# Four plain pairs instead of six, a packed block and closings set aside: one change to a weight-gradient kernel

## The chip, the cores and the metric

The kernel runs on one NeuronCore of a Trainium2 chip. The engines named here are TensorE (PE: matmuls, and PEld: its weight loads), VectorE (DVE), ScalarE (ACT), GpSimd (POOL) and SyncE (SP). The metric is the device time of one execution in microseconds (us), from runs of which the median counts.

## What is computed

```
batch, m, k, n = 16, 512, 1024, 768
grad_weight = np.einsum('bmk,bmn->kn', input, grad_output)     # float32 in, float32 out
```

Batch and m together are one contraction over 8192 rows: out (1024 x 768) = X^T G, with X (8192 x 1024) and G (8192 x 768).

## The kernel before

**Pairs.** The 8192 rows are cut into 32 pairs u = 0 to 31 of 256 rows each. A pair's X and G come by DMA from GpSimd's queue, which turns f32 into bf16 on the way; only the first 128 rows (and the X of the second 128) come as f32 on the queues of SP and ACT and are rounded on the chip (round_by). From pair 3 on (MERGED) a pair is one DMA for G (L159) and one for X (L160); earlier pairs come in halves (L164, L166). The pool "pairs" has room for 14 (PAIRS_HELD).

**Blocks.** The output is cut into four blocks: A (first half of K, left half of N), B (first half of K, right), C (second half of K, left), D (second half of K, right). Each is 512 x 384 and is made of four row groups q of 128 x 384, called A0 to A3 and so on.

**Plain and Winograd pairs.** LOADS gives the kind of every pair. A plain pair ("s") is two items of 128 rows, and each item costs one matmul (128 x 128 weights, 384 moving columns) for each of the 16 row groups: 32 matmuls. A pair of the other kind ("P") is treated as a 2 x 2 by 2 x 2 block product by the Winograd form of Strassen's scheme: 7 products instead of 8, 28 matmuls. Its products are collected in A, B and C and in four shared sums called 1, 5, 6 and 7, each with four row groups as well. It needs six sums on DVE ahead of its products: sum_x stages 0, 1, 2 (L190, L192, L194) and sum_g stages 0, 1, 2 (L200, L202, L204), in the order that the plan gives. Their results xe and ge lie in the pool "sums" (SUMS_HELD = 10). D collects only from plain pairs. At the end the shared sums are added into A, B, C and D (SHARED, and two subtractions at the closing of 5).

**Banks.** PSUM has eight banks. A row group that is being collected occupies one. Those that are not have their running sum in SBUF: acc for A to D, macc for 1, 5, 6 and 7. A row group comes back in one of two ways: ACT copies its running sum into a bank (fill, L281) and the matmuls add to it there, or it starts from zero and its closing adds. A closing takes it out: ACT copies (L334), DVE copies (L336), or DVE adds the bank to the running sum (L338). The last closing of a row group adds a shared sum on DVE (L318, L314, L315) and stores it to DRAM, on SP's queue. The very last block is filled in two banks, 256 and 128 columns, so that its first piece can be closed while the second is multiplied; the 256-column piece is stored on ACT's queue.

**Order.** PE, DVE, ACT and GpSimd run in the order of the program, and that is the order of PLAN, a list of 1069 tokens written out by hand or by a planner. `A3@1.2`: two matmuls of A3, opened in bank 1. `C0.1`: one more of C0. `fB2@1`: fill B2 into bank 1. `vA3`, `cA2`: close by DVE or by ACT. `g1.6`, `x0.6`: a stage of the sums of pair 6. `r0`: a rounding of the first rows. The loop at the end of the function (L343 to L359) issues the tokens one by one. In this plan four row groups at a time stay in their banks over long stretches (A0, A1, C0, C1 at first), and banks 1, 2, 6 and 7 rotate.

Of the kernel before, what the change touches and what calls it, by code (L numbers as in the profile page):

```python
# [9 lines left out]
P = 128  # L10

LOADS = "ssssssPPPPPPPPPPPPPPPPPPPPPPPPPs"
# [10 lines left out]
    "A0@0.1 A3@1.1 A2@2.1 C3@7.1 vA3 C2@6.1 cA2 C0@4.1 C1@5.1 r0 cC3 A1@3.1 vC2 B2@1.1 D2@2.1 D1@7.1 cB2 "  # L23
    "r1 D3@6.1 r2 r3 vD2 D0@1.2 r4 A0.1 vD3 C1.1 cD1 B1@2.2 vD0 A1.1 B3@7.2 cB1 B0@6.2 vB3 D1@1.1 D2@2.1 "
    "cB0 C0.1 vD1 A3@7.2 fC2@6 vD2 C1.1 A1.1 fB2@1 A0.1 vA3 C2.2 C3@2.2 cC2 A2@7.2 vC3 B2.2 fD3@6 C0.1 "
    "vA2 D2@2.2 cB2 D3.3 vD2 B1@1.2 cD3 B0@7.2 vB1 D0@2.2 fD1@6 C0.1 vB0 C1.1 fB3@1 D1.3 vD0 fA3@7 B3.3 "
    "vD1 A3.2 cB3 C3@6.2 vA3 C2@2.2 fA2@1 A0.2 vC3 fB2@7 A2.3 vC2 fB0@6 B2.3 vA2 B0.2 vB2 fD3@1 D2@2.2 "
    "A1.3 vB0 fB1@7 vD2 D3.2 fD0@6 B1.2 cD3 B3@2.1 D0.2 vB1 fA3@1 C1.2 vB3 C0.2 cD0 A3.1 fD1@7 C2@2.1 "
    "C3@6.1 vA3 A0.3 vC2 fA2@1 D1.3 vC3 A3@2.2 cD1 A2.2 vA3 B0@6.2 fB1@7 A1.2 vA2 fB2@2 B1.2 vB0 B3@1.2 "
    "cB1 B2.2 vB3 C2@6.2 fC3@7 C0.2 vB2 fD0@1 C3.2 vC2 D2@2.2 cC3 D0.2 vD2 D3@6.2 fA2@7 C1.4 vD0 fA3@2 "  # L30
    "vD3 fB0@1 A2.2 A3.2 cA2 B1@6.2 vA3 B0.2 fB2@7 A0.2 vB1 cB0 B3@2.2 fC2@6 B2.2 vB3 C3@1.2 cB2 A1.2 vC3 "
    "fD2@2 C0.2 C2.2 fD1@7 D2.4 fB1@1 vC2 D1.4 cD2 D3@6.4 cD1 D0@2.1 g0.6 D0.3 vD3 A1.2 B1.1 g1.6 fB0@6 "
    "B1.1 vD0 A2@7.2 cB1 C0.1 g2.6 C0.1 A0.2 fA3@2 vA2 C1.2 fB3@1 x0.6 C1.1 A3.3 fC2@7 B0.1 x1.6 B0.1 cA3 "
    "C2.2 x2.6 cB0 C2.1 B3.3 vC2 fC3@6 B2@2.2 g0.7 cB3 B2.1 C3.3 fB0@7 vB2 C0.1 fA2@1 A1.1 g1.7 73@2.1 "
    "vC3 B0.1 A2.1 c73 A0.1 vB0 11@6.1 cA2 13@2.1 g2.7 13.1 c11 10@7.1 x0.7 10.1 12@1.2 c13 71@6.1 v10 "
    "A0.1 c12 50@2.2 v71 51@7.2 c50 72@1.1 x1.7 72.1 c51 70@6.1 g0.8 70.1 63@2.1 c72 x2.7 63.1 A1.1 c70 "
    "C0.1 g1.8 11@1.1 v63 C1.1 fA2@7 60@6.2 g2.8 62@2.2 v11 c60 A2.2 c62 x0.8 A1.1 C2@1.2 cA2 C3@6.2 x1.8 "
    "52@2.3 vC2 53@7.2 x2.8 c52 53.1 61@1.1 g0.9 61.2 c53 A0.1 vC3 fB1@2 C1.1 A3@7.1 g1.9 A3.1 c61 C0.1 "
    "B1.3 vA3 f13@6 B0@1.1 g2.9 B0.1 cB1 73@7.2 x0.9 13.2 f12@2 C1.1 v73 A1.1 c13 12.2 x1.9 C0.1 f71@6 "
    "50@7.2 vB0 A0.1 c12 71.1 x2.9 71.2 f72@1 g0.10 B2@2.3 c71 v50 72.2 fB3@6 g1.10 63@7.2 c72 vB2 B3.2 "  # L40
    "g2.10 B3.1 11@2.3 v63 cB3 10@1.1 x0.10 fC3@7 10.2 A0.1 fA2@6 v11 C1.1 C3.2 x1.10 A2.2 f51@2 v10 A1.1 "
    "C0.1 cC3 51.1 g0.11 51.2 cA2 60@1.1 x2.10 60.2 f70@7 g1.11 62@6.3 c51 v60 70.2 g2.11 fC2@1 70.1 v62 "
    "A3@2.3 c70 x0.11 C2.3 f73@6 A0.1 vA3 f53@7 73.2 cC2 x1.11 73.1 53.3 v73 f52@1 61@2.2 x2.11 c53 61.1 "
    "52.1 g0.12 fB1@6 52.2 C0.1 v61 fB0@7 C1.1 B1.1 g1.12 B1.2 c52 B0.1 g2.12 B0.2 cB1 12@1.2 x0.12 cB0 "
    "12.1 13@2.3 f71@6 v12 A1.2 f72@7 x1.12 71.3 f50@1 v13 72.2 c71 x2.12 72.1 50.1 g0.13 f63@2 50.2 A0.1 "
    "c72 B2@6.3 v50 fB3@7 63.1 g1.13 63.2 vB2 fA2@1 B3.2 g2.13 c63 B3.1 A2.1 x0.13 A2.2 fC3@6 C0.2 cB3 "
    "vA2 C1.2 10@2.1 f11@7 x1.13 10.2 f51@1 C3.1 x2.13 C3.2 g0.14 11.3 cC3 v10 51.3 c11 g1.14 70@6.3 "
    "f60@2 v51 A0.1 f62@7 A1.1 g2.14 60.3 v70 fA3@1 62.1 x0.14 62.2 c60 A3.3 fC2@6 v62 52@2.2 x1.14 cA3 "
    "52.1 C2.2 f53@7 x2.14 C2.1 A0.1 g0.15 f73@1 A1.1 53.3 cC2 v52 73.1 g1.15 73.2 f61@6 v53 B0@2.3 c73 "
    "g2.15 61.3 fB1@7 vB0 C0.1 f12@1 C1.1 x0.15 C1.1 c61 B1.3 f13@2 x1.15 12.3 vB1 50@6.2 c12 x2.15 50.1 "  # L50
    "13.1 g0.16 fB3@7 13.2 A0.1 f72@1 v50 A1.1 B3.2 c13 g1.16 B3.1 72.1 g2.16 72.2 cB3 10@2.2 c72 71@6.3 "
    "v10 fB2@1 C3@7.2 x0.16 C3.1 f63@2 B2.3 v71 63.2 cB2 x1.16 63.1 A0.1 vC3 C0.2 c63 60@6.1 x2.16 f11@1 "
    "60.2 g0.17 A1.1 fA2@2 C1.1 11.3 v60 f51@7 A2.1 g1.17 A2.2 c11 g2.17 51.3 cA2 x0.17 70@6.3 c51 62@1.3 "
    "fA3@2 v70 C0.1 fC2@7 C1.1 x1.17 A3.3 f73@6 v62 C2.2 x2.17 cA3 C2.1 73.1 g0.18 f61@1 73.2 vC2 A1.1 "
    "fB0@2 A0.1 61.1 c73 g1.18 61.2 B0.1 fB1@7 g2.18 B0.2 v61 52@6.2 cB0 x0.18 52.1 B1.3 f12@1 v52 A1.1 "
    "f53@2 C0.1 12.1 x1.18 cB1 12.2 53.1 f13@6 x2.18 53.2 g0.19 c12 53.1 13.3 v53 fB2@1 71@7.2 g1.19 c13 "
    "71.1 B2.1 g2.19 B2.2 f10@2 v71 B3@6.3 cB2 10.2 fC3@7 x0.19 10.2 f50@1 A0.2 vB3 c10 C3.2 x1.19 C3.1 "
    "f72@6 50.4 vC3 72.1 g0.20 f70@7 72.3 x2.19 c50 63@2.2 g1.20 c72 63.2 g2.20 70.3 f11@6 v63 60@1.3 v70 "
    "fA2@2 11.2 x0.20 f51@7 11.2 C1.3 v60 c11 A2.1 x1.20 A2.3 x2.20 51.2 cA2 g0.21 51.2 62@1.4 fC2@2 v51 "
    "A3@6.1 g1.21 f52@7 A3.2 v62 C2.3 vA3 f73@1 52.2 g2.21 cC2 52.1 A1.1 x0.21 A1.2 f61@6 C0.3 v52 fB0@2 "  # L60
    "73.1 x1.21 73.3 fB1@7 x2.21 61.2 c73 g0.22 61.2 B0.4 f12@1 v61 B1.1 g1.22 f13@6 B1.3 vB0 12.1 g2.22 "
    "12.2 cB1 13.1 x0.22 13.3 c12 f71@7 53@2.4 v13 fB2@1 71.1 x1.22 fB3@6 71.3 v53 B2.2 x2.22 c71 B2.1 "
    "B3.1 g0.23 fC3@2 B3.3 vB2 f10@7 A0.2 cB3 g1.23 A0.1 C1.2 f72@1 g2.23 10.3 70@6.1 x0.23 70.2 c10 C3.4 "
    "v70 f50@7 72.1 x1.23 f60@6 72.3 vC3 50.2 g0.24 c72 50.2 f63@2 x2.23 60.3 g1.24 c50 60.1 63.1 g2.24 "
    "63.3 c60 A3@1.3 v63 A1.2 x0.24 f52@2 A1.1 C0.3 vA3 C2@7.2 x1.24 C2.2 f11@1 52.1 x2.24 52.3 vC2 "
    "A2@6.2 c52 g0.25 A2.2 f51@7 11.4 vA2 f62@2 51.1 g1.25 f12@6 51.3 v11 62.1 g2.25 62.2 c51 x0.25 62.1 "
    "f73@1 C1.3 v62 f13@7 12.2 x1.25 12.2 A0.1 x2.25 A0.2 c12 g0.26 73.4 f61@6 g1.26 B0@2.3 c73 g2.26 "
    "B0.1 13.3 vB0 61.4 v13 fB3@2 B1@1.1 x0.26 B1.3 c61 C0.1 f53@6 x1.26 C0.1 A3@7.3 vB1 B3.1 x2.26 B3.2 "
    "fB2@1 g0.27 53.4 cB3 vA3 B2.2 f10@2 g1.27 B2.2 c53 g2.27 B2.1 71@7.4 cB2 f70@6 10.1 x0.27 10.4 fC3@1 "
    "v71 70.3 c10 x1.27 70.2 72@2.1 x2.27 72.2 c70 g0.28 72.1 C3.4 f50@6 v72 A1.1 g1.28 f63@2 A1.2 vC3 "  # L70
    "50.2 g2.28 50.2 f11@1 60@7.4 v50 C1.1 x0.28 fA2@6 C1.2 A0.3 v60 11.1 x1.28 11.3 fC2@7 x2.28 63.2 c11 "
    "g0.29 63.3 f51@1 A2.1 g1.29 A2.2 c63 g2.29 A2.1 51.4 vA2 52@2.4 v51 C2.1 x0.29 f62@1 C2.4 v52 12@6.2 "
    "cC2 x1.29 12.2 f13@2 62.1 g0.30 62.3 f73@7 x2.29 62.1 13.1 g1.30 13.3 c62 v12 C0.1 f10@1 g2.30 C0.2 "
    "v13 73.4 f11@6 f12@2 x0.30 10.3 c73 11.1 x1.30 11.1 c10 12.1 A1.3 v11 f13@7 A0.2 v12 f60@1 13.1 "
    "f61@6 x2.30 C1.2 60.3 v13 f62@2 61.5 f63@7 v60 f70@1 63.2 v61 62.1 C0.1 70.3 v63 f71@6 v62 A0.2 "
    "f72@7 A1.2 v70 f73@2 C0.2 vA0 71.4 f50@1 vA1 fA2@0 72.3 vC0 fA3@3 A2.4 v71 f51@4 C1.2 v72 fC2@6 A3.6 "
    "vA2 f52@7 vC1 50.3 vA3 C2.3 v50 fB0@0 52.2 fD0@3 B0.7 vC2 v52 fB2@1 51.2 fD2@5 B2.6 vB0 v51 fD1@6 "
    "73.1 D0.2 fB1@0 D2.2 vB2 B1.7 v73 f53@4 fC3@1 vD0 53.4 vD2 vB1 C3.5 v53 fD3@2 D1.2 fB3@0+7 D3.2 vC3 "
    "B3.7 vD1 vD3 vB3 "
# [4 lines left out]
PAIRS_HELD = 14  # L84
SUMS_HELD = 10

MERGED = 3
# [7 lines left out]
def kernel(  # L95
# [31 lines left out]
    SLOT = {"1": 0, "5": 1, "6": 2, "7": 3}  # L127

# [142 lines left out]

    def fill(p, q, b, b2):
        assert (p, q) not in opened and not fresh[p, q] and b in used
        src = sum_of(p, q)
        if b2 is None:
            parts = [(bank(b), 0, NH)]
        else:
            assert b2 in used
            parts = [(bank(b), 0, 256), (bank(b2), 256, NH)]
        for tile_, c0, c1 in parts:  # L280
            nc.scalar.copy(out=tile_[:, 0 : c1 - c0], in_=src[:, c0:c1])  # L281
        opened[p, q] = (parts, True)

    def multiply(p, q, b, n):
        first = (p, q) not in opened
        if first:
            opened[p, q] = ([(bank(b), 0, NH)], False)
            used.add(b)
        parts, carried = opened[p, q]
        for tile_, c0, c1 in parts:  # L290
            for j in range(n):
# [8 lines left out]
                    skip_group_check=True,  # L300
                )
        done[p, q] += n

    def close(engine, p, q):
        parts, carried = opened.pop((p, q))
        final = done[p, q] == len(streams[p])
# [85 lines left out]
```

## Time and profile before

| what | value |
|---|---|
| median of 3 runs (lowest, highest) | 162.13 us (161.96, 162.14) |
| the profiled execution | 162.41 us |
| its span, first to last instruction | 160.6 us |
| PE, DVE, ACT, POOL busy | 156.1, 141.9, 124.2, 35.7 us |
| matmuls on data / with their weights | 931 (917 of 384 columns, 7 of 256, 7 of 128) |
| first and last data matmul start | 5.18 and 156.72 us |
| fills by ACT | 163 of 384 columns or in pieces of 256 and 128 |
| data moved, HBM read | 33.40 MB, 58.72 MB |

The profiled execution is one of its own: a span of 160.6 us and 1.8 us around it. Times inside it are counted from its first instruction. Busy shares are means over the whole span. A matmul's duration in the profile is from its start until its result is out, so durations of successive matmuls overlap, and the pace has to be read from start to start; the same holds for DVE and ACT, whose successive instructions overlap by some 0.1 us. GpSimd's busy time here is its issue of the DMAs.

### The profile page before, as it was taken

The numbers are of one execution on the slowest core, as the hardware profiler recorded it, in microseconds if no ns is written. First come the engines' busy times: TensorE is split into PE (matmuls) and PEld (weight loads), VectorE is DVE, ScalarE is ACT, GpSimd is POOL, SyncE is SP. The second block draws the span as 40 slices with busy tenths as digits, with TensorE's granted clock in tenths as the row PEclk, the third lists the DMA queues.
The fourth block names the chain that finished last, engine by engine and source line by source line (L and its number), as shares of the span: only waits on it lengthen the run. The fifth ranks groups of instructions, "written<-read, shape, count | busy, mean of one in ns | idle before, by whom it ended". The sixth has DMA issues, their size and how long they took to land.

```text
span 160.6 us, 2815 instructions
## 1 busy us (share of the span) xinstructions
PE 156.1 (97%) x937; PEld 92.4 (58%) x937; DVE 141.9 (88%) x322; ACT 124.2 (77%) x282; POOL 35.7 (22%) x71
## 2 busy tenths in 40 slices
PE   8999999999999999999999999999999999999990
PEld 3355566565565555665556556656655655665560
DVE  0788898698999999999889999998999899999992
ACT  3677878969879899898899986898576855989540
POOL 7445221222212222222122222122222100000000
PEclk9999999999999999999999999999999999999999
DMA  4999999999999999999999999999999999923865
GB/s 160 302 208 213 214 216 211 212 213 213 216 210 212 211 212 213 216 211 211 217 214 213 212 211 213 211 214 213 211 214 213 213 214 213 215 49 77 280 231 196
DMA packets 12734, 33.40 MB, mean 208 GB/s; under 512 B 1456, under 2 KB 4528, under 8 KB 12720
## 3 DMA queue, kind: packets, MB, share of 16 engines
q0 software_dynamic: 9648, 28.64, 90.4%
q1 hardware_dynamic: 2640, 3.41, 6.6%
q10 hardware_dynamic: 432, 1.18, 2.0%
q8 instruction: 7, 0.11, 0.3%
q14 instruction: 7, 0.06, 0.1%
HBM read 58.72 MB, written 3.15 MB: 385 GB/s over the span
## 4 chain that ended last, share of the span: by engine, by line
PE 95%; DVE 2%; issue 1%; ACT 0%; DVEq 0%
PE bank L294 92%; PE bank L142 3%; DVE acc L318 1%; ACT acc L334 0%; DVE macc L314 0%; DVEq L387 0%; DVE macc L315 0%
## 5 line engine op out<-in xcount | busy, mean ns | idle before, releaser
L294 PE MATMUL bank<-gp,xp 128*128 128x384 bf16 (+2 forms) x631 | 111.8, 325 | 0.1
L294 PEld LDWEIGHTS <-xp 128*128 128x128 bf16 x631 | 61.6, 98 | 42.4 <-DVE xp L208 1.6
L294 PE MATMUL bank<-ge,xe 128*128 128x384 bf16 x300 | 58.0, 326 | 0.0
L281 ACT COPY bank<-acc 128x384 f32<-128x384 f32 (+1 forms) x82 | 38.0, 480 | 7.8 <-DVE acc L318 2.0
L281 ACT COPY bank<-macc 128x384 f32<-128x384 f32 x82 | 38.6, 485 | 6.1 <-DVE macc L336 2.7
L294 PEld LDWEIGHTS <-xe 128*128 128x128 bf16 x300 | 29.3, 98 | 19.6
L334 ACT COPY macc<-bank 128x384 f32<-128x384 f32 x61 | 28.6, 480 | 6.0 <-PE bank L294 4.6
L334 ACT COPY acc<-bank 128x384 f32<-128x384 f32 x51 | 24.1, 479 | 7.9 <-PE bank L294 7.1
L160 POOL DMA_DIRECT2D xp<-in_input_dram x29 | 15.3, 527 | 51.0 <-DMA xp<-in_input_dram 27.7
L338 DVE TENSOR_TENSOR acc<-bank,acc 128x384 f32<-128x384 f32 x45 | 24.3, 553 | 2.0 <-PE bank L294 1.3
L159 POOL DMA_DIRECT2D gp<-in_grad_output_dram x29 | 15.3, 527 | 36.4 <-DMA gp<-in_grad_output_dram 16.5
L336 DVE COPY acc<-bank 128x384 f32<-128x384 f32 x30 | 16.2, 554 | 3.7 <-PE bank L294 3.1
L338 DVE TENSOR_TENSOR macc<-bank,macc 128x384 f32<-128x384 f32 x32 | 17.7, 554 | 1.6 <-PE bank L294 1.5
L190 DVE TENSOR_TENSOR xe<-xp 128x1024 bf16<-128x1024 bf16 x25 | 17.1, 684 | 0.0
L336 DVE COPY macc<-bank 128x384 f32<-128x384 f32 x25 | 13.7, 555 | 1.7 <-PE bank L294 1.2
L200 DVE TENSOR_TENSOR ge<-gp 128x768 bf16<-128x768 bf16 x25 | 13.8, 553 | 0.7 <-DMA gp<-in_grad_output_dram 0.7
L194 DVE TENSOR_TENSOR xp<-xp,xe 128x512 bf16<-128x512 bf16 x25 | 10.5, 421 | 0.3
L192 DVE TENSOR_TENSOR xe<-xe,xp 128x512 bf16<-128x512 bf16 x25 | 10.5, 419 | 0.2
L204 DVE TENSOR_TENSOR gp<-ge,gp 128x384 bf16<-128x384 bf16 x25 | 8.8, 353 | 0.4
L202 DVE TENSOR_TENSOR ge<-gp,ge 128x384 bf16<-128x384 bf16 x25 | 8.8, 352 | 0.1
L318 DVE TENSOR_TENSOR acc<-bank,macc 128x384 f32<-128x384 f32 (+2 forms) x17 | 8.2, 524 | 0.0
L208 DVE CAST gp<-gf 128x192 bf16<-128x192 f32 (+1 forms) x2 | 0.6, 306 | 4.6 <-DMA gf<-in_grad_output_dram 4.6
(17 smaller groups left out, 24.5 us busy)
## 6 DMA issues: line engine op xcount, KB each, us to landing
xp<-in_input_dram POOLq DMA_DIRECT2D x29, 512.0 KB, 16.8
gp<-in_grad_output_dram POOLq DMA_DIRECT2D x29, 384.0 KB, 16.8
out_dram<-acc SPq DMA_DIRECT2D x12, 192.0 KB, 2.0
xf<-in_input_dram ACTq DMA_DIRECT2D x2, 512.0 KB, 5.1
xp<-in_input_dram POOLq DMA_DIRECT2D x4, 256.0 KB, 8.5
gp<-in_grad_output_dram POOLq DMA_DIRECT2D x5, 192.0 KB, 7.7
out_dram<-acc SPq DMA_DIRECT2D x6, 96.0 KB, 2.2
gf<-in_grad_output_dram SPq DMA_DIRECT2D x2, 192.0 KB, 4.4
```

The lines of the kernel that those rows point to most:

```text
L159: nc.gpsimd.dma_start(out=gp, in_=G[rows, :].rearrange("(p m) n -> p m n", m=2))
L160: nc.gpsimd.dma_start(out=xp, in_=X[rows, :].rearrange("(p m) k -> p m k", m=2))
L190: nc.vector.tensor_sub(out=xe[:, 0:2, :], in0=x[:, 1::-1, :], in1=x[:, 3::-2, :])
L192: nc.vector.tensor_sub(out=xe[:, 2, :], in0=xe[:, 0, :], in1=x[:, 0, :])
L194: nc.vector.tensor_add(out=x[:, 1, :], in0=x[:, 2, :], in1=xe[:, 2, :])
L200: nc.vector.tensor_add(out=ge[:, 0:2, :], in0=g[:, 0:2, :], in1=g[:, 1::2, :])
L281: nc.scalar.copy(out=tile_[:, 0 : c1 - c0], in_=src[:, c0:c1])
L294: nc.tensor.matmul(tile_[:, 0 : c1 - c0], stat, mov[:, c0:c1], start=first and j == 0, stop=True, skip_group_check=True,)
L318: nc.vector.tensor_add(out=dst[:, c0:c1], in0=b, in1=sum_of(SHARED[p], q)[:, c0:c1])
L334: nc.scalar.copy(out=dst, in_=b)
L336: nc.vector.tensor_copy(out=dst, in_=b)
L338: nc.vector.tensor_add(out=dst, in0=b, in1=dst)
```

## The change

- LOADS has 4 plain pairs in front instead of 6, and 27 Winograd pairs instead of 25; the last pair stays plain. MERGED goes from 3 to 2, so pair 2 comes in two DMAs as well. PAIRS_HELD goes from 14 to 10, SUMS_HELD from 10 to 8.
- A's four row groups, 4 x 384 = 1536 columns, are packed into banks 0, 1 and 2 (3 x 512 columns) and stay there from their first matmul to their last (PACKED, PLACES). A1 and A2 each lie across two banks, so each of their steps is two matmuls with the same weights, of 128 and 256 columns. C0 keeps bank 3, and banks 4 to 7 rotate. The flag that clears a bank is set only on the first matmul in it.
- A new kind of closing, `zcC3.0` or `zvC2.1` (set_aside): ACT or DVE copies the bank to one of 20 new SBUF places instead of adding to the running sum, and a later token `yC3.0` (add_aside) has DVE add that place to the running sum. There are 35 of each; 30 of the copies are on ACT and 5 on DVE.
- A new token `wC1` (merge): GpSimd adds a shared sum to a running sum in SBUF, ahead of the row group's last fill, so that its last closing is a plain copy, on ACT (`cC1`). There are three: C1, B1 and B3.
- The plan is new throughout (1087 tokens). It has 121 fills instead of 163. On DVE it has 91 adding closings and 16 copies, where there were 77 and 52; on ACT it has 109 copying closings of the old kinds, where there were 112. The very last block is B2 instead of B3, still in two pieces.

```diff
-LOADS = "ssssssPPPPPPPPPPPPPPPPPPPPPPPPPs"
+LOADS = "ssssPPPPPPPPPPPPPPPPPPPPPPPPPPPs"
...
-PAIRS_HELD = 14
-SUMS_HELD = 10
-
-MERGED = 3
+PAIRS_HELD = 10
+SUMS_HELD = 8
+ASIDE = 20
+
+MERGED = 2
+PACKED = True
+PLACES = {
+    0: [(0, 0, 0, 384)],
+    1: [(0, 384, 0, 128), (1, 0, 128, 384)],
+    2: [(1, 256, 0, 256), (2, 0, 256, 384)],
+    3: [(2, 128, 0, 384)],
+}
...
+    aside = [accp.tile([P, NH], f32, name=f"aside{i}") for i in range(ASIDE)]
...
+        if first and PACKED and p == "A":
+            parts = []
+            for nb, t0, c0, c1 in PLACES[q]:
+                if nb not in packed:
+                    packed[nb] = bank(nb)
+                    used.add(nb)
+                parts.append((packed[nb], t0, c0, c1))
+            opened[p, q] = (parts, False)
...
+        for i, (tile_, t0, c0, c1) in enumerate(parts):
             for j in range(n):
                 at = done[p, q] + j
                 stat, mov = operands(p, streams[p][at], q)
+                start = first and j == 0
+                if start and PACKED and p == "A":
+                    nb = PLACES[q][i][0]
+                    start = nb not in begun
+                    begun.add(nb)
                 nc.tensor.matmul(
-                    tile_[:, 0 : c1 - c0],
+                    tile_[:, t0 : t0 + c1 - c0],
                     stat,
                     mov[:, c0:c1],
-                    start=first and j == 0,
+                    start=start,
...
+    def set_aside(engine, p, q, i):
+        ((b, t0, _, _),), carried = opened.pop((p, q))
+        assert not carried and not fresh[p, q] and done[p, q] < len(streams[p])
+        copy = nc.vector.tensor_copy if engine == "v" else nc.scalar.copy
+        copy(out=aside[i], in_=b[:, t0 : t0 + NH])
+        laid.add((p, q, i))
...
+    def add_aside(p, q, i):
+        laid.remove((p, q, i))
+        assert (p, q) not in opened or not opened[p, q][1]
+        dst = sum_of(p, q)
+        nc.vector.tensor_add(out=dst, in0=dst, in1=aside[i])
+
+    def merge(p, q):
+        assert (SHARED[p], q) in closed and (p not in "BD" or ("5", q) in closed)
+        assert (p, q) not in opened and not fresh[p, q] and (p, q) not in closed
+        merged.add((p, q))
+        dst = sum_of(p, q)
+        nc.gpsimd.tensor_add(out=dst, in0=dst, in1=sum_of(SHARED[p], q))
```

In the new close, a row group for which merge has run is copied like any other instead of being added to a shared sum, and a copy by ACT of a piece of 128 columns of a split row group goes to DVE.

## The prediction

> **What bounds the kernel now.** I read the page first, then the groups with their forms kept apart, the timelines of TensorE (PE), VectorE (DVE) and GpSimd, and last the stretches.
>
> ```profile
> PE 156.1 (97%) x937; PEld 92.4 (58%) x937; DVE 141.9 (88%) x322; ACT 124.2 (77%) x282; POOL 35.7 (22%) x71
> ...
> PE   8999999999999999999999999999999999999990
> ...
> DMA  4999999999999999999999999999999999923865
> ```
>
> Two things are full at once: PE until the end, and the DMA engines until slice 36. The forms and the timeline give the true pace of PE:
>
> ```profile
> L294 PE MATMUL bank<-gp,xp 128*128 128x384 bf16 x617 | 110.6, 327 | 0.1
> ...
> L294 PE MATMUL bank<-gp,xp 128*128 128x256 bf16 x7 | 0.9, 272 | 0.0
> ...
> L294 PE MATMUL bank<-gp,xp 128*128 128x128 bf16 x7 | 0.6, 219 | 0.0
> ```
> ```profile
> 145.93 2.11 PE L294 MATMUL bank<-gp,xp 128*128 128x384 bf16 x12
> ...
> 154.21 2.78 PE L294 MATMUL bank<-gp,xp 128*128 128x384 bf16 x23
> ```
>
> Durations overlap. Twelve matmuls start in 2.11 - 0.33 us, so one costs 0.1625 us. The second row holds 9 full ones, 7 of 256 columns and 7 of 128 (merged under the first one's form): their starts stand 0.1625, 0.109 and 0.056 us apart, and 9x0.1625 + 7x0.109 + 6x0.056 + 0.219 = 2.78. So a matmul cut in 256 + 128 columns costs 0.0025 us more than a whole one. PE runs from 5.18 to 156.78 us; its work is 924x0.1625 + 7x0.0025 = 150.17 us, and 1.43 us are small gaps. 0.8 of them fall before 8 us.
>
> DVE comes next:
>
> ```profile
> 52.15 0.55 DVE L338 TENSOR_TENSOR macc<-bank,macc 128x384 f32<-128x384 f32 x1
> 52.61 0.69 DVE L190 TENSOR_TENSOR xe<-xp 128x1024 bf16<-128x1024 bf16 x1
> 53.21 0.55 DVE L338 TENSOR_TENSOR macc<-bank,macc 128x384 f32<-128x384 f32 x1
> 53.68 0.42 DVE L192 TENSOR_TENSOR xe<-xe,xp 128x512 bf16<-128x512 bf16 x1
> 54.01 0.55 DVE L338 TENSOR_TENSOR macc<-bank,macc 128x384 f32<-128x384 f32 x1
> 54.48 0.55 DVE L200 TENSOR_TENSOR ge<-gp 128x768 bf16<-128x768 bf16 x1
> ```
>
> From start to start a closing of a bank costs 0.467 us, L190 0.600, L192 and L194 0.333 each, L200 0.467, and (other rows of this view) L202 and L204 0.266 each: 2.265 us for the six sums of a Winograd pair. In this stretch DVE has no pause.
>
> The input sets the earliest time for all of it. GpSimd issues it, each DMA when the eighth before it has landed:
>
> ```profile
> 117.17 0.53 POOL L160 DMA_DIRECT2D xp<-in_input_dram  x1 [1.94 <-DVE ge L202]
> ...
> 121.49 0.53 POOL L160 DMA_DIRECT2D xp<-in_input_dram  x1 [1.89 <-DMA xp<-in_input_dram]
> ...
> 125.80 0.53 POOL L160 DMA_DIRECT2D xp<-in_input_dram  x1 [1.94 <-DVE gp L204]
> ```
>
> A pair takes 4.31 us. The last lands 16.9 us after 125.80, at 142.71; PE first touches it at 143.98 and has 12.8 us of work from there to 156.78.
>
> **PE's sum.** I counted both plans by token. By position I mean the matmul time that stands ahead of a token, at the paces above. Before: 7 plain pairs of 32 matmuls and 25 Winograd pairs of 28, 924. After: 5x32 + 27x28 = 916. Cut ones: A1 and A2 now straddle banks, 37 steps each, and the last block has 7: 81. Work after: 916x0.1625 + 81x0.0025 = 149.05 us, **1.12 less**. Weight loads double for cut steps, but the 128-column row already has one load per 0.056 us, so they hide.
>
> **The input's cap.** Neither bytes nor their order change, and the engines are full, so I keep the landings (merging the third pair delays its first tile to 16.4 us; the plan first touches it at position 10.4, about 16.6 us). After its first use of the last pair the new plan has 13.19 us of PE work: end not before 142.71 + 13.19 + about 0.1 of hand-over = 156.0, so the **gain is 0.78 at most**. Pairs 22 and 24, reckoned likewise, give 155.90 and 155.79 without the hand-over, nearly the same.
>
> **Fewer buffers.** With 10 pairs held, pair u waits for pair u-10. By positions its last use is never less than 24.6 us ahead of pair u's landing, and the issue comes 17.3 us ahead: 7 us of cover. Were it gone, DMA would idle and the cap would move one for one. Sums with 8 buffers: the nearest reuse is 14.5 us away. Both cost nothing.
>
> **DVE's sum.** Closings on DVE fall (77 adds and 52 copies become 91 adds, 16 copies and 5 settings-aside), but 12 sums and 35 additions of a set-aside place (add_aside, both inputs f32 in SBUF) come. That last form is not in the trace. Bounds: 0.266 (the bf16 add of its shape, L202) and 0.600 (the longest add, L190). The bf16 rows rise 0.522 ns per element over a fixed 0.066 us; the f32 add from PSUM, 0.467, is that fixed part plus 384 elements at twice the rate. So I take 0.467. [...]
>
> At 0.467, from position 10 to 120 us DVE has before 103 closings and 130 sums, 97.3 us; after 88 closings, 32 additions and 143 sums, 110.1 us, **in 110 us of PE time**. Worst stretch: positions 20 to 70 hold 309 matmuls, 50.2 us, and 38 closings, 14 additions and 70 sums, 50.96 us. DVE comes 0.75 us later out of it than into it, and never gets that back before 120. Its queue is in order: behind each late instruction wait bank closings, ACT's refills after them, and the sums that the next products read. I charge the whole **0.75 to PE**. ACT falls from 109.7 to 102.5 us (refill 0.414, copy 0.376 start to start); its fullest 10 us hold 9.1. The packing makes this possible: A's blocks have no refills left.
>
> **GpSimd's three additions.** The trace has none. Ends: 0.10 us (its MEMSET row, 101 ns) and 1.83 (DVE's add, 0.553, plus a one-off load as long as ACT's table load, 1.283). I take 0.55, by DVE's row of the same shape. Tightest is B1: its shared sum is ready about 143.3 in position, its refill stands at 144.16, so 0.9 us is hidden; above that the refill, and behind it all of ACT's queue, is late one for one, 0.9 at the upper end. The other two have 1.6 and more. GpSimd's DMAs are all issued by 126 us, so nothing is queued behind these adds. [...]
>
> **Start and tail.** The gap of 0.24 us at 7.52 us (a bank waiting for its copy) may go; the input and DVE bind later, so I count nothing. At the end both plans have three whole additions and the last block in two pieces behind the same number of matmuls, with stores on the same two queues: nothing.
>
> **Sum.** -1.12 + 0.75 = -0.37, inside the cap. Profiled execution: 162.41 - 0.37 = 162.04, a span of 160.2; it lies 0.28 above the median of the three runs, so 162.13 - 0.37 = **161.8**. Own range 161.4 to 162.2.
>
> **Rivals.**
> - *DVE does not bind*: additions cheaper, or late closings covered by other banks. For it: before, with DVE nearly full from 40 to 60 us, PE's gaps after 8 us sum to only 0.6. Against it: 110.1 us in 110. The input's cap then decides: 162.13 - 0.78 = 161.35.
> - *DVE overflows*, the other side: the addition costs more than I take. Place: positions 10 to 120, with 32 of them. Each 0.01 us gives 0.32 us, undiminished, since DVE has no slack there; from 0.487 (0.02 x 32 = 0.64) it is slower by more than the measurement's bound. Midway to the upper end, 0.533: 161.8 + 2.1 = 163.9. For it: every reading of two f32 tensors from SBUF is unseen here. Against it: L190 to L204 read two SBUF tensors at the expected pace while GpSimd issues DMAs.
> - *GpSimd late* at the upper end: 161.8 + 0.9 = 162.7.
> - *The packing doesn't do what it says*: cut matmuls, alternating 128 and 256 instead of seven alike, show weight loads. Bound: 74 steps of at most one load row, 0.098 us, less 0.056, 3.1 us: 164.9.
>
> **Chances.** Forecast 0.52, DVE free 0.16, DVE overflow 0.22, GpSimd 0.06, packing 0.04. A measurement of this kernel tells 0.2% (0.32 us) from no change. The forecast lies at that bound, so I split it 0.27 faster and 0.25 within. Faster 0.27 + 0.16 = 0.43. Within: 0.25 and 0.02 of GpSimd, 0.27. Slower: 0.22 + 0.04 + 0.04 = 0.30. The range reaches from the cap to the overflow: 161.3 to 163.9; outside lie the packing, the dearest additions and something unseen.
>
> **What would show it.** PE: starts 0.056 and 0.109 apart in A1 and A2, and 149.05 us of work. DVE: idle nearly nothing from 25 to 125 us, the add_aside row at 0.55 long and 0.467 from start to start. Input: last landing at 142.7, PE less than 1.2 us behind it. GpSimd: three rows under 0.9 us, no ACT refill waiting for them. The forecast is wrong if PE's gaps after 8 us sum to over 2 us (overflow) or stay under 1.0 (DVE free).

## The result, and the profile after

The changed kernel takes 162.69 us (median of 9 runs, 162.43 to 162.88), the kernel before 162.03 us in the same comparison (9 runs, 161.93 to 162.61). The ratio is 1.0031, with a 95% interval from 1.0021 to 1.0041: slower by 0.3%, where 0.2% faster was forecast. The profiled execution took 162.59 us, with a span of 160.8 us and 1.8 us around it as before.

The same rows of the page, after:

```profile
span 160.8 us, 2956 instructions
...
PE 155.2 (97%) x1003; PEld 95.2 (59%) x1003; DVE 148.6 (92%) x351; ACT 116.8 (73%) x267; POOL 37.7 (23%) x72
...
PE   8999999999999999999999999999999999999980
...
DVE  0599999999999999999999999999999999979990
...
DMA  5999999999999999999999999999999999914766
```

PE has 66 more matmuls and yet less busy time; its last slice but one has gone from 9 to 8. DVE is full from the third slice to the 35th. DMA falls to 1 in slice 36, when the input has ended (2 before). So the work is out of PE earlier, and what has grown lies behind it. The groups with their forms kept apart (line, engine, operation, tiles, shapes, count | busy us, mean ns) show the parts of the change one by one:

```profile
L328 PE MATMUL bank<-gp,xp 128*128 128x384 bf16 x511 | 95.6, 326 | 0.3 <-DVE xp L224 0.2
...
L328 PE MATMUL bank<-ge,xe 128*128 128x384 bf16 x324 | 62.5, 326 | 0.0
...
L328 PE MATMUL bank<-gp,xp 128*128 128x256 bf16 x81 | 15.7, 273 | 0.0
...
L328 PE MATMUL bank<-gp,xp 128*128 128x128 bf16 x81 | 12.1, 219 | 0.0
...
L392 DVE TENSOR_TENSOR acc<-acc,aside 128x384 f32<-128x384 f32 x21 | 11.6, 562 | 0.0
...
L399 POOL TENSOR_TENSOR acc<-acc,macc 128x384 f32<-128x384 f32 x3 | 3.0, 1002 | 22.2 <-DVE macc L364 19.9 <-DVE macc L359 2.4
```

835 whole matmuls and 81 cut ones: the counts of the prediction. An addition of a set-aside place is 562 ns long, one on GpSimd 1002 ns. Now the end. These rows are the timeline of the changed kernel's last 6 us (start, length, engine, line, operation, tiles, count):

```profile
153.31 2.77 PEld L328 LDWEIGHTS <-xp 128*128 128x128 bf16 x23
153.47 2.78 PE L328 MATMUL bank<-gp,xp 128*128 128x384 bf16 x23
...
154.64 2.01 DVE L364 TENSOR_TENSOR acc<-bank,macc 128x384 f32<-128x384 f32 x5
156.48 0.39 ACTq L346 DMA_DIRECT2D out_dram<-acc  x1
```

The 23 matmuls run as dense as before (again 2.78 us), and the last closing ends at 154.64 + 2.01 = 156.65. Before, the last of the closings ended at 157.60. From there on the two kernels part:

| us | before | after | after - before |
|---|---|---|---|
| last data matmul starts | 156.78 | 156.03 | -0.75 |
| last closing ends | 157.60 | 156.65 | -0.95 |
| SP issues its last store at | 157.62 | 157.59 | -0.03 |
| last store lands | 159.69 | 159.89 | +0.20 |
| span ends | 160.61 | 160.80 | +0.19 |

(The table of the profile before gives 156.72 for the last matmul; that is the start of the last but one.) Before, SP issues the last store 0.02 us after the last closing; after, 0.94 us later. All that PE and DVE gained is lost behind the last closings. The stores by themselves (engine, line, count: shortest/median/longest issue in ns, first and last start):

```profile
L346 SPq DMA_DIRECT2D out_dram<-acc x9: 332/405/1289, 152.8 to 157.6; - x9
L346 ACTq DMA_DIRECT2D out_dram<-acc x1: 386/386/386, 156.5 to 156.5; - x1
```

One issue took 1.289 us: that of 153.25, of a whole row group like its neighbours. The seven behind it then follow back to back, 0.48 to 0.50 us apart from 154.63 to 157.59. In the page of before the queue list has 7 packets of kind "instruction"; after, it has 8:

```profile
q8 instruction: 8, 0.13, 0.3%
```

Columns: packets, MB, share of 16 engines. Each packet of q8 has 16384 bytes. Before, they start at 22.71, 43.93, 64.26, 85.25, 105.68, 125.57 and 144.26 us; after, at 21.13, 40.34, 59.89, 79.03, 98.78, 117.97, 136.48 and **152.95**, and the last one takes 1.21 us. It lies on the stopped store. A view of the DMA queues cut to the microsecond from 152 shows the packet in place:

```profile
q8 instruction: 1, 0.02, 7.6%
```

7.6% of 16 engines' microsecond is 1.21 us of one engine: the packet holds one of the 16 for its whole length.

Whose instructions are these? The packets keep step with PE's matmuls, not with time. After the first they come every 115 to 129 matmuls before and every 108 to 131 after, though this is 18.7 to 21.2 us in the one and 16.5 to 19.8 us in the other. So I read each of them as a fetch of PE's own instructions. No row names the engine; f1 below, which adds 25 matmuls and 25 weight loads on PE and no instruction on DVE, ACT or GpSimd, moves the last packet from 152.95 to 149.56.

**Theory 1.** The changed plan has 66 matmuls and weight loads more, so PE's eighth fetch comes before the end, in the middle of the stores. The fetch stops SP's queue and costs about 1 us. **Theory 2.** The tail's closings are bunched by the new order: too many stores at once. **Theory 3.** SP's own pace of one store in 0.46 to 0.50 us is the limit. And for the stage ahead of the tail: does **DVE** hold PE back, as the prediction charged?

### The profile page after: what moved, and what is told of

Same layout as the page of the kernel before. It is cut to its first block, busy times and chain, and to the rows that moved or that the text cites. A ratio compares the mean times of both kernels' runs of the same rounds, so it can differ in the third digit from the quotient of the medians.

```text
span 160.8 us, 2956 instructions
## 1 busy us (share of the span) xinstructions
PE 155.2 (97%) x1003; PEld 95.2 (59%) x1003; DVE 148.6 (92%) x351; ACT 116.8 (73%) x267; POOL 37.7 (23%) x72
## 3 DMA queue, kind: packets, MB, share of 16 engines
q10 hardware_dynamic: 432, 1.18, 2.0%
## 4 chain that ended last, share of the span: by engine, by line
PE 93%; DMA 3%; DVE 1%; issue 0%; DVEq 0%
PE bank L328 93%; DMA xf<-in_input_dram 3%; DVE acc L364 1%; DVE xp L224 0%; DVEq L364 0%
## 5 line engine op out<-in xcount | busy, mean ns | idle before, releaser
L328 PE MATMUL bank<-gp,xp 128*128 128x384 bf16 (+2 forms) x673 | 107.1, 307 | 0.3 <-DVE xp L224 0.2
L328 PE MATMUL bank<-ge,xe 128*128 128x384 bf16 x324 | 62.5, 326 | 0.0
L367 ACT COPY macc<-bank 128x384 f32<-128x384 f32 x71 | 33.1, 480 | 12.5 <-PE bank L328 11.5
L371 DVE TENSOR_TENSOR acc<-bank,acc 128x384 f32<-128x384 f32 x48 | 26.0, 562 | 0.5 <-PE bank L328 0.2
L371 DVE TENSOR_TENSOR macc<-bank,macc 128x384 f32<-128x384 f32 x43 | 24.7, 573 | 0.0
L302 ACT COPY bank<-acc 128x384 f32<-128x384 f32 (+2 forms) x42 | 19.4, 476 | 3.1 <-DVE acc L371 1.3
L367 ACT COPY acc<-bank 128x384 f32<-128x384 f32 x38 | 17.9, 479 | 5.0 <-PE bank L328 4.7
L383 ACT COPY aside<-bank 128x384 f32<-128x384 f32 x30 | 13.3, 483 | 3.8 <-PE bank L328 3.7
L392 DVE TENSOR_TENSOR acc<-acc,aside 128x384 f32<-128x384 f32 x21 | 11.6, 562 | 0.0
L392 DVE TENSOR_TENSOR macc<-macc,aside 128x384 f32<-128x384 f32 x14 | 8.2, 583 | 0.0
L399 POOL TENSOR_TENSOR acc<-acc,macc 128x384 f32<-128x384 f32 x3 | 3.0, 1002 | 22.2 <-DVE macc L364 19.9
```

Source lines behind the costliest of these rows:

```text
L302: nc.scalar.copy(out=tile_[:, t0 : t0 + c1 - c0], in_=sum_of(p, q)[:, c0:c1])
L328: nc.tensor.matmul(tile_[:, t0 : t0 + c1 - c0], stat, mov[:, c0:c1], start=start, stop=True, skip_group_check=True,)
L367: nc.scalar.copy(out=d, in_=b)
L371: nc.vector.tensor_add(out=d, in0=b, in1=d)
L383: copy(out=aside[i], in_=b[:, t0 : t0 + NH])
L392: nc.vector.tensor_add(out=dst, in0=dst, in1=aside[i])
```

## The experiments

All ratios are against the kernel before, measured together with the run, with the 95% interval.

### More cut matmuls (e1)

The fetch is moved out of the tail by more PE instructions: all of A's row groups are cut, 74 matmuls more (and A0 and A3 are closed in two pieces, as A1 and A2 are).

```diff
-    0: [(0, 0, 0, 384)],
+    0: [(0, 0, 0, 128), (0, 128, 128, 384)],
...
-    3: [(2, 128, 0, 384)],
+    3: [(2, 128, 0, 128), (2, 256, 128, 384)],
```

> The changed kernel, with A0 and A3 cut into 128 and 256 columns as well: 74 more matmuls, 0.19 us more work for PE (74 x 0.0025), nothing else moved. In the changed kernel's profile one packet of 16384 bytes on the instruction queue starts at 152.95 us and takes 1.21 us; SP's store issued at 153.25 takes 1.29 us instead of 0.33, and the later ones follow one behind the other, the last 0.94 us after its data are ready. These packets come every 19 us, about 118 full matmuls. Theory 1 (PE's instruction fetch collides with the stores): 74 more matmuls bring the fetch 74 x 0.1625 = 12 us forward, to about 141, where no store is under way; no SP store over 0.5 us, the time falls by 0.85 and rises by 0.19: 162.0. Theory 2 (seven stores in the last 3 us are too many for the queue or the DMA engines, whatever the fetch): the time rises by 0.19, to 162.9.

Measured: 162.79 us, 1.0022 (1.0006 to 1.0038). No gain in sum, but two effects can be seen in the trace. The last fetch comes at 144.32, no store stops, and from the last closing to the end of the span there are 3.28 us (157.67 to 160.95), where the changed kernel has 4.15 and the kernel before 3.01. In exchange PE loses time early; its timeline near 20 us, with the wait and its releaser in brackets:

```profile
18.79 2.12 PE L328 MATMUL bank<-gp,xp 128*128 128x384 bf16 x14
21.92 2.29 PE L328 MATMUL bank<-gp,xp 128*128 128x384 bf16 x13 [1.01 <-DMA xp<-in_input_dram]
```

PE stands 1.17 us at 20.6 us for the X of a pair, and the input's last landing goes from 142.69 to 143.15. The first fetch has moved too, from 21.13 to 19.82, just ahead of that landing. A DMA lands in 16 parts, as many as there are DMA engines; of this X 15 had landed by 20.43 and the last one came at 21.87, where in the changed kernel all 16 had landed by 20.73. That it is this fetch which holds the one part up fits but was not tested alone. So theory 1 was neither upheld nor refuted by the time: the fetches must be moved late only.

### Two stores on another queue (e2)

```diff
-                store(p, q, 0, NH, nc.sync)
+                store(p, q, 0, NH, nc.scalar if (p, q) in (("D", 1), ("D", 2)) else nc.sync)
```

> The changed kernel, with the stores of D1 and D2 issued by ACT, which has nothing left to do there. Theory 3 (SP's issue pace of 0.49 us a store is what makes the last one late): SP has two stores fewer ahead of the last one, which leaves at about 156.7 instead of 157.59; the time falls by 0.8, to 161.9. Theory 2 in the form that the bytes are the limit (landings stand 0.53 us apart for 192 KB): landings stay where they are, 162.6 to 162.7. Theory 1: one of 16 DMA engines is behind by the fetch and holds every landing up, so at most 0.3 less.

Measured: 162.70 us, 1.0025 (1.0016 to 1.0035): as slow as without the edit. SP's last store is now issued at 156.74 instead of 157.59, but the last landing stays at 159.89. The store at 153.31 is stopped as before, for 1.19 us. Theory 3 falls: the landings stay where they are, whichever queue issues the stores. Theory 2, in the form that the bytes are the limit, had forecast just this as well, so e2 doesn't tell it from theory 1.

### Other orders of the tail (e3, f2)

e3 moves the closings of D1, D0 and D3 and the products of shared sum 5 so that closings come more evenly; f2 does it again, without the PE wait that e3 made. From `fD3@7` on, with changed tokens only in their places:

```
after: C2.6 cC1 wB3 vC3 fB1@0 D3.2 v50 fB0@2 B1.5 fD0@1 vC2 B0.4 fB3@5 vD3 cB1 52.3 vB0 B3.3 v52 fD2@0 D1.2 fB2@2+4 D0.2 cB3 D2.2 vD1 B2.7 vD0 vD2 vB2
e3:    D1.2 C2.6 cC1 wB3 vC3 vD1 fB1@0 D3.2 v50 fB0@2 B1.5 fD0@1 vC2 52.3 vD3 B0.4 fB3@5 cB1 D0.2 v52 vB0 B3.3 vD0 fD2@0 fB2@2+4 cB3 D2.2 B2.7 vD2 vB2
f2:    D1.2 C2.6 cC1 wB3 vC3 vD1 fB1@0 D3.2 v50 fB0@2 52.3 fD0@1 vC2 B1.5 fD2@3 vD3 fB3@5 v52 B0.4 cB1 fB2@7+4 D0.2 vB0 D2.2 vD0 B3.3 vD2 cB3 B2.7 vB2
```

> The changed kernel with the last 60 or so matmuls in another order, the same work: D1 and D0 are finished earlier and 52 ahead of B0, so that four whole stores instead of six and the two pieces fall in the last 3 us of PE. The fetch stays where it is. Theory 2 (bunched stores): the last store is not queued behind others, 0.85 less: 161.85. Theory 1: the fetch still stops SP for 0.9 us, but behind it SP has pauses to catch up, so nearly the same, 161.85 to 162.2. If it stays at 162.7, neither the bunching nor the fetch makes the tail long.

Measured e3: 162.59 us, 1.0018 (1.0009 to 1.0028). PE waits 0.70 us at 154.7 for a bank, so the order itself costs something, and the test is not clean.

> The changed kernel with the last 60 matmuls in an order whose last two refills go to banks 3 and 7 + 4, free early, so that PE does not stand as it did 0.70 us in the first reordering. Two whole stores fewer come behind the fetch at 153. Theory 2: each is worth 0.53 us (landings stand 0.53 apart), 1.0 us less, 161.7. Theory 1 says nearly the same, since the stores behind the fetch drain at that pace: 161.7 to 162.0. If PE's order costs it time again, its gaps after 150 us say how much.

Measured f2: 162.57 us, 1.0028 (1.0018 to 1.0038). PE has no gap in the tail, its last matmul starts at 155.93, and the last closing ends at 156.55. The stores of f2:

```profile
L344 SPq DMA_DIRECT2D out_dram<-acc x9: 332/403/1292, 151.8 to 157.7; - x9
```

Again one issue of 1.29 us, again beside a fetch (152.95, 1.67 us), and the last landing is at 159.85. Theory 2 asked for 1 us less and got 0.1, and theory 1's 161.7 to 162.0 was missed too. f3 below shows that this order has a price of its own, so what decides against theory 2 is f1, which keeps the order.

### The kernel before with more matmuls (e4)

60 matmuls of A0 and C0 are cut in the old plan, so that it gets an eighth fetch as well.

```diff
+                cut = q == 0 and (p == "A" or p == "C" and at < CUTS) and c1 - c0 == NH
+                for e0, e1 in [(c0, c0 + 128), (c0 + 128, c1)] if cut else [(c0, c1)]:
```

> The kernel before, with A0's and 21 of C0's steps cut into 128 and 256 columns: 60 more matmuls, 0.15 us more work. In its profile the fetches come at 22.7, 43.9, 64.3, 85.3, 105.7, 125.6 and 144.26 us; the next would come at about 165, after the end. Theory 1: 60 more matmuls bring it forward by 9.8 us to about 155.4, into the last five stores; one SP store takes over 1 us and the time rises by 0.15 plus 0.3 to 0.8, to 162.5 or more. Theories 2 and 3: only 0.15 more, 162.2.

Measured: 162.40 us (162.09 to 163.53), 1.0016 (0.9998 to 1.0034): unclear. The eighth fetch came at 155.69 and lasted until 156.57; one store was issued in it, in its last 0.13 us, and took the usual 0.33 us. So the stopped store that theory 1 forecast didn't come. The last landing is 2.97 us behind the last closing, where the kernel before has 2.09. For the nine stores from 153 us on (eight on SP, one on ACT) the view of this run has:

```profile
DMA to landing us min/median/max: 1.8/2.9/3.8
```

The same view of the kernel before has 1.8/2.0/2.1, with the issues on SP as short (332/342/376 ns against 332/342/371). The trace tells why: each of the last eight stores has 15 of its 16 parts on time and one late, by 1.96 us at first and by 0.86 at the end (159.98 and 160.84). So in the old plan, too, a fetch beside the stores holds the end up by 0.9 us, through one part in 16, and without SP being stopped. This profile is of the slowest of the 12 runs; how many of the others it speaks for is not known.

### Cuts late in the kernel only (f1)

The clean form of e1: only A0 is cut, and only from its 13th item on. 25 matmuls more, 0.0025 us each, all later than the early stage that e1 disturbed.

```diff
+CUT_FROM = 12
...
+                cut = (p, q) == ("A", 0) and at >= CUT_FROM
+                for e0, e1 in [(c0, c0 + 128), (c0 + 128, c1)] if cut else [(c0, c1)]:
```

> The changed kernel, with A0's steps cut into 128 and 256 columns from its 13th item on: 25 more matmuls, 0.06 us more work. The run with 74 more cuts showed the fetch leave the stores (tail from the last closing to the end 3.28 us instead of 4.16), but an earlier fetch then fell on the input of pair 3 and PE stood 1.17 us at 20.6 us. Here the cuts come late, so the fetches up to about 60 us stay where they are and the last one comes 25 x 0.1625 = 4 us earlier, at about 148.9, where SP has pauses between the stores. Theory 1: no long SP store after 150, PE as in the changed kernel, 162.7 - 0.85 + 0.06 = 161.9. Theory 2 (too many bytes in the last 3 us, whatever the fetch): 162.75.

Measured: **161.66 us** (161.61 to 161.87), 0.9972 (0.9962 to 0.9981): faster than both kernels, with more instructions on PE and all else alike. The page and the store rows:

```profile
PE 155.4 (97%) x1028; PEld 97.2 (61%) x1028; DVE 148.7 (93%) x351; ACT 116.6 (73%) x267; POOL 37.6 (24%) x72
```
```profile
L349 SPq DMA_DIRECT2D out_dram<-acc x9: 332/402/416, 152.8 to 156.7; - x9
```

The last fetch has gone from 152.95 to 149.56. No issue in the tail is longer than 0.42 us. PE's last matmul starts at 156.02 and the last closing ends at 156.64, both within 0.01 us of the changed kernel; but SP's last store is issued at 156.75 and lands at 159.00, 0.89 us earlier. The store that now lies beside the fetch, at 149.67, took 1.18 us; nobody waits for it there. From the last closing to the end of the span there are 3.26 us: 0.89 less than in the changed kernel, and 0.25 more than in the kernel before.

What the stop does shows in the busy time of the stores' DMA queue (packets, MB, share of 16 engines) in the microsecond from 154, first in the changed kernel, then in f1:

```profile
q1 hardware_dynamic: 58, 0.07, 20.6%
```
```profile
q1 hardware_dynamic: 267, 0.36, 102.2%
```

In the changed kernel the DMA engines stand nearly empty there, though closed blocks are ready; from 155 on both kernels move stores without a pause to the end, one landing every 0.53 us, so nothing can be made up. The kernel before still had pauses in its tail (31.2% in the microsecond from 156). The bunched closings of theory 2 are thus what leaves no room, and the 0.25 us may be theirs; the 0.89 us goes with the fetch alone. Theory 1 is upheld.

### Both (f3)

f1's cuts and f2's order together: is anything left for theory 2?

> The late cuts and the second order of the tail together. Theory 1: without a fetch among the stores the end follows the last closing by 3.0 us as in the kernel before, so the order adds nothing, 161.9. Theory 2: as with the order alone plus 0.06, 161.75; if the two gains add up, 161.0, both theories are incomplete.

Measured: 162.32 us, 1.0012 (1.0002 to 1.0022), 0.66 us more than f1. No store is stopped after 151 us (longest issue 0.43 us). What SP waited for from 152 us on (its line, whom it waited for, us in total, times, longest):

```profile
SPq L347 <- ACT acc L368: 1.0, 1, 1.0
```

This row is the price of the order: SP stands for B1's store until ACT has closed it at 155.49, with B0's, ready at 155.00, behind it. The last store goes out at 157.41 instead of 156.75. The more even order is the worse one, once the fetch is gone. Neither theory's time was met, as neither had this wait. Against f2 the moved fetch is worth only 0.25 us here, since this order has a pause in which most of the stop is made up.

### The set-aside additions left out (f4)

The 35 additions on DVE are not done: their parts of the sums are missing from the output. DVE has 35 x 0.467 = 16.3 us less to do.

```diff
-            add_aside(rest[0], int(rest[1]), int(rest[3:]))
+            laid.remove((rest[0], int(rest[1]), int(rest[3:])))
```

> The changed kernel without its 35 additions of set-aside places (these parts of the sums are left out of the output): 16.3 us less work for VectorE. PE's gaps between 25 and 52 us sum to 0.81 us in the changed kernel. If VectorE's load is behind them, as the prediction had it, they go and PE ends up to 0.7 us earlier, not before the input's cap of 155.9 + 0.1; in time 0.1 to 0.3 less, as PE was at 156.03 already. If the input or the order of the banks is behind them, they stay as they are and the time too.

Measured: 162.56 us, 1.0024 (1.0012 to 1.0036), nothing gained. Its busy row, and DVE's slices:

```profile
PE 155.3 (97%) x1003; PEld 95.1 (59%) x1003; DVE 138.0 (86%) x316; ACT 116.9 (73%) x267; POOL 37.6 (23%) x72
...
DVE  0699868988899999989899988989899988869990
```

DVE has pauses everywhere, and still PE's last matmul starts at 156.08, and its gaps from 9 us on sum to 1.37 us, against 1.15 with the additions. Between 25 and 52 us DVE stands for 2.9 us, where with the additions it had no pause, and PE's gaps there are 0.79 us as against 0.81. The load of the additions did not hold PE back.

### More load on DVE (g4)

f1 with 12 more additions on DVE, whose results nobody reads, between 75 and 117 us: 12 x 0.467 = 5.6 us.

```diff
+        if (p, q, i) in AGAIN:
+            nc.vector.tensor_add(out=aside[i], in0=aside[i], in1=aside[i])
```

> The kernel with 25 late cuts, with one more addition of the same kind behind 12 of the additions between 75 and 117 us (it doubles the place just used, which nothing reads any more): 12 x 0.467 = 5.6 us more for VectorE, which is busy without a pause there. Taking all 35 additions out left PE as it was, so VectorE did not bind; this asks how near the edge it was. If it is full, each addition reaches PE: 161.7 + 5.6 less what lateness the banks still cover, 165 or more. If there is cover of 1 to 2 us for each and the plan's pauses catch it up, 161.7 to 162.2.

Measured: 168.56 us, 1.0411 (1.0391 to 1.0431), 6.9 us more than f1. The stretches (from:to, length, then busy us and count of PE, PEld, DVE, ACT, POOL; clock, DMA share, GB/s) of g4 and of f1:

```profile
60.00:100.00 40.00, 39.32 (x268) 24.89 (x266) 39.84 (x95) 33.58 (x78) 9.72 (x19) 1.00 1.07 213
100.00:140.00 40.00, 36.35 (x236) 21.66 (x234) 39.72 (x94) 18.84 (x42) 6.63 (x13) 1.00 1.07 213
```
```profile
60.00:100.00 40.00, 40.00 (x275) 25.53 (x274) 39.97 (x97) 34.55 (x80) 9.62 (x19) 1.00 1.07 213
100.00:140.00 40.00, 40.00 (x273) 25.50 (x272) 39.72 (x95) 23.59 (x53) 6.74 (x13) 1.00 1.07 213
```

In f1 PE has no pause in these 80 us; in g4 it does 44 matmuls fewer in the same time. So DVE is near its edge in this plan: 16.3 us less bring no gain, and 5.6 us more come out at the end in full. Why 6.9 us come out and not 5.6 was not settled.

### The buffers alone (g1)

The kernel before with the new pool sizes, `PAIRS_HELD = 10` and `SUMS_HELD = 8`.

> The kernel before with 10 pairs and 8 sums held instead of 14 and 10, nothing else. The prediction puts both at nothing, with 7 us of cover for the pairs: 162.1, landings as before, the last at 142.7. If the fewer buffers held the input back, the last landing would be later than 142.8 and the time above 162.4. It is also a second profile of the old plan: its PE end (156.78 in the first, taken from an execution 0.28 above the median) shows how much of PE's 0.75 us is the plan's.

Measured: 162.17 us, 1.0006 (0.9995 to 1.0018): no difference. The last input landed at 142.82.

### Ten cuts only (g2)

f1 with `CUT_FROM = 27`: only the last ten steps of A0 are cut, to put the fetch between the two places.

> The changed kernel with only the last 10 steps of A0 cut: the last fetch comes 1.6 us earlier, at about 151.3, in place of 152.95 (no cuts, 162.6) or 149.56 (25 cuts, 161.66). Theory 1: there SP has a pause of 1.0 us between the stores at 151.4 and 152.8 in which most of the stop is made up; between the two, nearer to the lower, 161.7 to 162.1, and a store of about 1.2 us. If only the number of cuts mattered, 10 of 25 would give 162.2 to 162.3.

Measured: 162.37 us, 1.0012 (1.0002 to 1.0021), between the two. But the fetch was not where it was expected: it came at 153.38 (0.88 us). The store beside it, at 153.70, took 0.94 us:

```profile
L349 SPq DMA_DIRECT2D out_dram<-acc x8: 343/402/935, 153.3 to 157.2; - x8
```

This stop is 0.35 us shorter than the changed kernel's, the span of the profile is 0.39 us shorter (160.41 against 160.80), and the median 0.32 us less. So the time goes by the length of the stop here, as far as two profiles can show it. When exactly a fetch comes I can't say from matmul counts: the last interval was 122 matmuls here, 108 in the changed kernel and 113 in f1.

### Without GpSimd's additions (g3)

f1 with the three merges taken out; C1, B1 and B3 are closed on DVE, as in the old manner.

```diff
-... f51@7 wC1 72.2 ... fC2@4 wB1 fD1@3 ... cC1 wB3 vC3 ... cB1 52.3 ... cB3 D2.2 ...
+... f51@7 72.2 ... fC2@4 fD1@3 ... vC1 vC3 ... vB1 52.3 ... vB3 D2.2 ...
```

> The kernel with 25 late cuts, without GpSimd's three additions: C1, B1 and B3 are closed by VectorE with the shared sum, as the others are. The prediction had these additions hidden, and they took 1.00 us each, with 0.096 us of waiting by PE ahead of B1. Taking them away frees that 0.1, and gives VectorE three closings more of 0.467 in its last 12 us, where it works 11.5: if it can take them, 161.55 to 161.7; if VectorE's queue is full there, the last closings come up to 0.5 later, 161.9 to 162.1.

Measured: 162.83 us, 1.0039 (1.0027 to 1.0051), 1.17 us more than f1 and more than either side expected. PE's last matmul starts at 156.10, nearly the same. DVE is what ends later:

```profile
155.39 2.47 DVE L367 TENSOR_TENSOR acc<-bank,macc 128x384 f32<-128x384 f32 x6
```

From 147 us on DVE has no pause, and its last closing ends at 157.86 instead of 156.64: 1.22 us later, for three closings more, 3 x 0.467 = 1.40 us.

### What the traces show together

In nine profiles a store of SP was issued during PE's last fetch and took longer than 0.9 us. In all nine it ended at the same distance behind the fetch:

| profile | fetch, start to end | store, start to end | behind the fetch |
|---|---|---|---|
| after | 152.95 to 154.16 | 153.25 to 154.54 | 0.38 |
| e2 | 153.13 to 154.13 | 153.31 to 154.50 | 0.37 |
| e3 | 152.97 to 154.60 | 153.69 to 154.99 | 0.39 |
| f1 | 149.56 to 150.49 | 149.67 to 150.85 | 0.36 |
| f2 | 152.95 to 154.62 | 153.71 to 155.00 | 0.38 |
| f3 | 149.37 to 150.60 | 149.61 to 150.97 | 0.37 |
| f4 | 153.30 to 154.26 | 153.30 to 154.62 | 0.36 |
| g2 | 153.38 to 154.26 | 153.70 to 154.64 | 0.38 |
| g3 | 149.37 to 151.00 | 149.61 to 151.37 | 0.37 |

The stop ends with the fetch. And in all nine the store issued just ahead of the stopped one landed in 15 parts on time and one late, 0.74 to 1.53 us behind the 15th (changed kernel: 154.63 and 155.53). A fetch thus holds up one of the 16 parts of what is stored beside it, as in e4, and a later store is stopped until it is over. In e3, f2 and g2 the first store after the fetch's start still took 0.33 or 0.34 us, and the second one was stopped; in e4 and g4 the only store that fell into a fetch came in its last 0.13 us or less (0.33 us in e4, 0.59 in g4). Why a fetch lets one store pass and stops the next is open: a queue that fills behind the one late engine would fit, but one store with a late part stands ahead of the stopped one in some profiles and two in others, and no run tests it.

## Why the prediction was wrong

**Start and tail: "with stores on the same two queues: nothing".** This is the step that failed. It counted closings, stores and queues, which are indeed alike, and left out the fetches of PE's instructions, which hold up the stores beside them (in the changed kernel one of a store's 16 parts, by 0.90 us, and the next store's issue, for 1.29). The prediction counted 81 cut matmuls at 0.0025 us each and said of their weight loads that they hide; that holds on PE (the starts of the 128-column ones stay 0.056 us apart), but as instructions they are 66 pairs more. The last one before is the 937th, after it is the 1003rd, and the eighth fetch came when 977 had started. Without it the plan gives 161.66 us (f1). The term was 0 and measures 0.9 to 1.0 us: 0.89 by the last landings, 1.03 by the medians of two comparisons (162.69 - 161.66), which also carries their scatter. From the last closing to the end of the span the profiles have 3.01 us before, 4.15 after and 3.26 in f1, so 0.25 us of the tail's growth is not the fetch's.

**PE's sum.** Right. Starts stand 0.1625, 0.109 and 0.056 us apart, counts are as predicted, and the packing does what it says.

**The input's cap.** Right: last landing at 142.69 (142.71 predicted from before), PE's end 156.03 (not before 156.0). PE took the cap's whole gain, 0.75 of 0.78. But the cap was used wrongly in the *DVE does not bind* rival: 0.78 was taken from the median of 162.13. A cap is a moment of the trace, and the profiled execution of before lay 0.28 above its median. From the moment itself, 156.0 + 3.83 (last matmul to the end of the span, before) + 1.80 (around the span) = 161.63; f1 measures 161.66. By this sum the lowest time in reach was about 161.6 and not 161.35, if the input lands as in the profiled execution.

**DVE's sum.** The load was right. Part of the changed kernel's timeline of DVE:

```profile
65.80 0.55 DVE L371 TENSOR_TENSOR macc<-bank,macc 128x384 f32<-128x384 f32 x1
66.27 0.42 DVE L208 TENSOR_TENSOR xe<-xe,xp 128x512 bf16<-128x512 bf16 x1
66.60 0.56 DVE L392 TENSOR_TENSOR acc<-acc,aside 128x384 f32<-128x384 f32 x1
67.07 0.42 DVE L210 TENSOR_TENSOR xp<-xp,xe 128x512 bf16<-128x512 bf16 x1
```

The closing L371, from a bank, and the addition L392, from SBUF, both hold the queue for 0.47 us, and DVE stands for 0.02 us in all from 25 to 125 us. What was wrong is the charge of 0.75 us to PE. Between PE's work saved, 1.12, and its end, 0.75 earlier, lie 0.27 us more of gaps and 0.10 of a later start, and f4 shows that the additions are not behind these gaps, since they stay without them. (After 8 us the changed kernel's sum to 1.27 us, between the two marks that the prediction had set, so the trace alone did not decide it.) The lateness that the worst stretch piles up did not reach PE; that other open banks covered it fits, but was not tested alone. g4 shows that the cover doesn't bear 5.6 us more. What the gaps between 28 and 52 us do come from was not settled; the trace puts one wait there, 0.17 us at 30.27, down to the input.

**The sum of -0.37** thus came out nearly right for f1 (161.66 against 161.8) by luck: a charge that was not there stands against a base that lay too low for the cap.

**Smaller readings**, without effect on the sum. PE's gaps before sum to 1.49 us and not 1.43, since 156.78 is where its last matmul starts, and 0.69 of them lie after 8 us, not 0.6. The *DVE overflows* rival crosses 0.32 us at 0.489 and not at 0.487. DVE's copies are 55 before and 19 after in the profiles, where 52 and 16 were counted.

**Fewer buffers.** Right (g1).

**GpSimd's three additions.** The price was 1.00 us instead of 0.55, within the ends given and over the 0.9 that the prediction had set as its sign; PE stood 0.096 us ahead of B1's first matmul, against 0.04 in g3, so the cover of 0.9 was nearly exact. The rows:

```profile
146.21 1.00 POOL L399 TENSOR_TENSOR acc<-acc,macc 128x384 f32<-128x384 f32 x1 [19.86 <-DVE macc L364]
149.59 1.97 POOL L399 TENSOR_TENSOR acc<-acc,macc 128x384 f32<-128x384 f32 x2 [2.38 <-DVE macc L359]
```

The first takes as long as the others: the one-off load in the prediction's upper end, 1.283 us, is not in it. Two MODIFY_POOL_CONFIG instructions of 0.04 us, which the kernel before and g3 don't have, stand on GpSimd at 126.35 us, 19.9 us ahead of the first addition, and GpSimd is idle in between; whether they stand for a load was not tested. What the prediction left out is the gain: it priced these additions as a risk and gave nothing for the three closings that DVE no longer adds. g3 puts that at 1.17 us.

**The rivals.** *DVE overflows* and the packing are refuted (no gaps over 0.1 us after 52 us; pace 0.056). *GpSimd late* gave 162.7, very near the measured time, but not by its mechanism. None named the tail.

## What to carry to other kernels

Count what a change adds in instructions, not only in time: in these traces packets of 16384 bytes came over the DMA engines every 108 to 131 matmuls, and one beside the last stores cost 0.89 us by the landings (f1) that no sum of engine times shows. In the trace, look for one issue much longer than its neighbours and for an "instruction" packet beside it, compare when the parts of a DMA landed, and move the fetch by a few dozen instructions before anything else is blamed. A full engine need not hold the end: take load away and put load on before charging it, and reckon with a cap as a moment in the trace, not as a difference from a median.

## What the runs showed of the hardware

- A fetch of 16384 bytes took 0.88 to 1.67 us, as one packet, which is the time of one DMA engine in 16. In nine profiles it stopped a store's issue, which then ended 0.36 to 0.39 us behind it; the store ahead of the stopped one had 15 parts on time and one late by 0.74 to 1.53 us.
- In the kernel before, the 16 parts of an input DMA on GpSimd's queue landed within 0.39 us of each other before the first fetch (the last of these DMAs at 22.15 to 22.50 us) and those of the next one within 1.35 us, 15 of them by 24.99 and one at 25.96. The late part is 0.97 us behind the 15th, where the fetch took 0.94. The late parts become more in the course of the run, three at 46 us (0.56, 1.27 and 1.32 behind the first part) and eight of 16 over 0.9 us at the last DMA of the input (141.08 to 142.71).
- A kernel became 1.0 us faster by 25 more instructions of each kind on PE (f1 against the changed kernel).
- GpSimd added 128 x 384 f32 from SBUF in 1.00 us; DVE's start-to-start time for the same shape is 0.467.
